# A mixture-of-experts kernel: the last expert's rows given to the tokens by one-hot products, the other rows' loads issued ahead of its work, and the row buffer zeroed in the mixer

## The chip, the cores and the metric

The kernel runs on one core of a Trainium2 chip. The metric is device time in microseconds (us) from launch to end of one execution; three executions of the kernel before gave 2562.1, 2564.21 and 2567.2 us, and the median, 2564.21 us, is the time that a change is held against. All arithmetic is float32, partly as products of split halves.

## What is computed

Two layers act on 512 latent tokens and 256 context tokens of 1024 columns. Each layer has a token mixer (windowed attention, a Fourier mix, a retention with chunks, three gates and an output projection) and then a mixture of 32 experts, of which each token uses two. The last layer drops the context tokens. Cut to the part that the change touches:

```python
def expert_ffn(xb, e, w_g, w_u, w_d):
    return (silu(xb @ w_g[e]) * (xb @ w_u[e])) @ w_d[e]        # 1024 -> 512 -> 1024

def hier_moe(h, ...):
    grp = argmax(h @ w_rg + b_rg)                              # one of 4 groups
    top_v, top_i = top_k(expert_logits_of_group, 2)            # two of its 8 experts
    w = p_grp * softmax(top_v)
    out[token] += w * expert_ffn(h[token], expert)             # for both experts of a token
x = x + g2 * hier_moe(modulate(rmsnorm(x), ...))
return rmsnorm(x, norm_final)                                  # after the second layer
```

## The kernel before, in words

The kernel is written with a tile framework that orders each engine's instructions by a schedule simulated ahead of time; the source gives the order in which the work has priority. Buffers come from pools: `unit` (20 buffers of 8 KB a partition, for weights, token rows and more), `W2` (7 of 2 KB), `raws` (4 of 2 KB), and eight PSUM banks in pools of three (`psm`), two (`pss`), two (`pst`) and one (`pso`). SP issues nearly all loads, in order.

In each layer the mixer comes first. Its projections read weights in pieces of 256 KB through `split_load` (L234). Around L760 attention ends, and the Fourier tables `t2` are loaded (L762 and L763).

Then comes the expert part. The router ranks the experts by their load, so that rank 0 has the most tokens. `SLOTS` (L31) gives each rank a fixed number of blocks of 32 rows; a pair makes one block of 64 rows. Rank 31 has one block of 32 in both layers. `prep` (L1067) builds a one-hot matrix of a rank's tokens, gets token numbers and weights by small products (`slots`, L1025), and gathers the tokens' rows from DRAM on the POOL queue. `wload` (L955) loads an expert's six weight tiles of 1 MB each, four of gate and up and two of down; a load is issued when the fourth load before it has landed.

The loop at L1198 goes over the experts in the order `seq` (L1191 to L1195): first rank 0 (ranks 0 and 1 in the second layer), then some of the smallest, then a small and a large one in turn, so that the last has a middle rank and two slots. For each block it runs `hidden` (L1143: gate and up products, then Silu on ACT and a product on DVE), `turn` of the block before (L1158: transposes and a copy), `take` of the block after (L1131), and `give` of the block before (L1167: the down product, the scaling by the routing weight and by `g2`, and a scatter of the 64 or 32 rows to `y_d` in DRAM, on the POOL queue). Each token has two rows in `y_d`, and both are written exactly once. After the loop the last block is turned and given (L1215), and in the first layer the decay tables of the second layer's retention are made (`decay_logs` and `decay_tables`, L1216 to L1218).

At L1222 stands a loop with a count read from memory, which gives a rank that has more tokens than slots its further blocks. With these inputs it is passed over. Every engine has a part in it.

At L1251 to L1268, for each tile `t` of 128 tokens (six in the first layer, four in the second): SP loads both rows of each token from `y_d` (`yb`, 1 MB), DVE adds them and adds the sum to `x`, ACT squares, DVE and POOL make the reciprocal root (`rstd_x`, L1270), and DVE scales. In the first layer the scaled rows go on to the second layer's `make_h` (L247), whose transposes stand at L259; in the second the result is stored to `out`.

Of the kernel before, what the change touches and what calls it, by code (L numbers as in the profile page):

```python
# [14 lines left out]
AF = mybir.ActivationFunctionType  # L15
# [10 lines left out]
NE = 32  # L26
# [4 lines left out]
SLOTS = ([4, 6, 5, 4, 4, 4] + [3] * 6 + [2] * 16 + [1] * 4, [3] * 2 + [4] * 4 + [3] * 3 + [2] * 8 + [1] * 15)  # L31
# [30 lines left out]
def tile_backbone(ctx: ExitStack, tc: tile.TileContext, a: dict, out: bass.AP, stop=None, dbg=None):  # L62
# [36 lines left out]
    def pst():  # L99
        return ps(pstr, "tr")  # L100
# [296 lines left out]
    def layer(l, xt_l, xt_c):  # L397
# [363 lines left out]
        o_tiles("F")  # L761
        t2 = unit("t2")  # L762
# [404 lines left out]
        def give(aT, sz, wd, di, ws):  # L1167
# [14 lines left out]
            DVE.scalar_tensor_tensor(y, p2[:, 0:n], ws[:, 0:1], g, op0=OP.mult, op1=OP.mult)  # L1182
            s = POOL.indirect_dma_start(out=y_d[l].rearrange("r (a c) -> (r a) c", c=n),  # L1183
# [7 lines left out]
        seq, rest = list(range(NS)), list(range(NS, NE))  # L1191
# [4 lines left out]
        last, xT = None, None  # L1196
        pre += [prep(r) for r in seq[NS:2]]
        for i, r in enumerate(seq):  # L1198
            e = r if r < NS else nc.values_load(oi[0:1, r:r + 1], engines=[ET.SP], min_val=0, max_val=NE - 1)
            w = wload(e) if i else first  # L1200
# [4 lines left out]
            for j, (xg, sz, di, ws) in enumerate(blocks):  # L1205
# [8 lines left out]
                last = (sg, sz, wd, di, ws)  # L1214
        give(turn(*last[:2]), *last[1:])  # L1215
        if full:  # L1216
            decay[1] = decay_logs(1)
            decay[1] = decay[1], decay_tables(*decay[1][0:2])  # L1218
# [31 lines left out]

        xs = {}  # L1251
        yv = y_d[l].rearrange("(k r h) c -> r k (h c)", k=2, h=2)
        for t in TL:
            yb = unit("yb").rearrange("p (k c) -> p k c", k=2)
            SP.dma_start(yb, yv[(t - t0) * 128:(t - t0) * 128 + 128])  # L1255
            x = xt[t]
            DVE.tensor_tensor(yb[:, 0], yb[:, 0], yb[:, 1], op=OP.add)  # L1257
            DVE.tensor_tensor(x, x, yb[:, 0], op=OP.add)
            if full and t >= 2:
                SP.dma_start(x_d[(t - 2) * 128:(t - 1) * 128, :], x)  # L1260
            ss = rstd_x(x, yb[:, 1])
            xs[t] = yb[:, 0]
            if full:
                DVE.tensor_scalar(xs[t], x, ss, None, op0=OP.mult)
            else:
                DVE.scalar_tensor_tensor(xs[t], x, ss, nf, op0=OP.mult, op1=OP.mult)  # L1266
                SP.dma_start(out[(t - 2) * 128:(t - 1) * 128, :], xs[t])
# [196 lines left out]
```

## Time and profile before

| | us |
|---|---|
| median of three executions | 2564.21 |
| lowest, highest | 2562.1, 2567.2 |
| the profiled execution's own time | 2571.19 |
| its span, first to last instruction | 2569.4 |
| TensorE busy (matmul) | 2354.5 (92%) |
| VectorE busy | 1019.1 (40%) |
| ScalarE busy | 576.1 (22%) |
| GpSimd busy | 544.6 (21%) |
| moved by DMA | 595.21 MB, mean 232 GB/s |
| mean granted TensorE clock | 0.956 |

PE is TensorE's matmuls and PEld its weight loads, DVE is VectorE, ACT ScalarE, POOL GpSimd, and SP the engine that issues most transfers; a q behind an engine's name is its queue, where it issues transfers and waits. The shares are means over stages with different limits: in the mixers PE is busy and the DMA engines are mostly idle, in the expert parts both are busy, and at the end of each expert part neither is. A matmul's end is modelled in the profile, so a busy PE may be a waiting one. The span is 1.8 us shorter than the profiled execution's own time, and that time is 7.0 us above the median of the three.

### The profile page before, as it was taken

The page shows a single profiled execution, that of the slowest core. Times are in us where ns is not written, and L with a number is a line of the kernel's source. Part 1 is how long each engine was busy: PE and PEld are TensorE (multiplying, and loading weights), DVE is VectorE, ACT ScalarE, POOL GpSimd, SP SyncE. Part 2 cuts the span into 40 slices and gives each one's busy share as a digit, 9 for nine tenths or more (in the row PEclk, how much of TensorE's full clock was granted, in tenths as well). Part 3 has the DMA queues.
Part 4 walks back from the last instruction along what each step waited for, and adds up shares of the span by engine and source line. Part 5 has one row for each costly group of instructions (what it writes and reads, how often), then busy time and mean ns, then how long its engine had stood idle before and what let it go on. Part 6 is the DMA issues. An engine that isn't in the chain of part 4 may idle for free. (4 is left out here: it accounts for less than half of the span.)

```text
span 2569.4 us, 44175 instructions
## 1 busy us (share of the span) xinstructions
PE 2354.5 (92%) x17341; PEld 1543.7 (60%) x17341; DVE 1019.1 (40%) x3007; ACT 576.1 (22%) x1269; POOL 544.6 (21%) x454
## 2 busy tenths in 40 slices
PE   5999999999999799999999599999999789988774
PEld 3788766888889643434443388768888643343221
DVE  5534555424334732333332745464334622221112
ACT  4222345211222201111110432354233200000000
POOL 0223233001223321111211233241122321121111
PEclk8999999999999799999999799999999799998887
DMA  7433100444333699899999522211335699999996
GB/s 272 166 128 134 64 26 29 164 144 176 107 112 111 238 405 408 348 362 389 416 419 405 199 62 71 69 38 42 98 95 195 240 405 417 412 409 414 409 419 249
DMA packets 130018, 595.21 MB, mean 232 GB/s; under 512 B 20972, under 2 KB 22084, under 8 KB 74256
## 3 DMA queue, kind: packets, MB, share of 16 engines
q1 hardware_dynamic: 115472, 562.70, 57.2%
q0 software_dynamic: 13376, 26.27, 2.7%
q8 instruction: 138, 2.26, 0.4%
q10 hardware_dynamic: 960, 3.39, 0.4%
q14 instruction: 72, 0.59, 0.1%
HBM read 580.53 MB, written 28.25 MB: 237 GB/s over the span
## 5 line engine op out<-in xcount | busy, mean ns | idle before, releaser
L1149 PE MATMUL mm<-w_gu,xT 128*32 128x256 f32 (+1 forms) x3776 | 569.7, 507 | 72.2 <-DMA w_gu<-in_w_gu_dram 69.5
L1149 PEld LDWEIGHTS mm<-w_gu,xT 128*32 128x32 f32 (+1 forms) x3776 | 194.9, 127 | 379.6 <-issue 236.1
L239 DVE TENSOR_TENSOR hl<-raw,hl 128x512 fp32r<-128x512 f32 x248 | 185.9, 751 | 270.9 <-ACT hl L238 270.1
L276 PE MATMUL mm<-hH,hl 128*128 128x512 f32 x720 | 286.2, 399 | 0.2 <-DVE shuf L317 0.2
L277 PE MATMUL mm<-hL,hl 128*128 128x512 f32 x720 | 284.1, 395 | 0.0
L278 PE MATMUL mm<-hH,hl 128*128 128x512 f32 x720 | 281.9, 392 | 1.2 <-DVE hl L239 1.2
L1174 PE MATMUL mm<-w_d,aT 128*32 128x256 f32 (+1 forms) x1888 | 267.8, 488 | 8.8 <-DVE aT L1164 7.7
L1183 POOL DMA_INDIRECT y_d<-y,gd x87 | 87.7, 1008 | 725.9 <-DVE y L1182 540.2
L238 ACT CAST hl<-raw 128x512 fp32r<-128x512 f32 x248 | 153.7, 621 | 384.8 <-PE mm L278 213.8
L1154 ACT ACTIVATE act<-mm 128x256 f32<-128x256 f32 (+1 forms) x87 | 30.1, 346 | 900.6 <-PE mm L1149 857.8
L1174 PEld LDWEIGHTS mm<-w_d,aT 128*32 128x32 f32 (+1 forms) x1888 | 92.8, 124 | 157.2 <-issue 122.2
L1155 DVE TENSOR_TENSOR act<-act,mm 128x256 f32<-128x256 f32 (+1 forms) x87 | 32.2, 370 | 367.0 <-ACT act L1154 364.9
L278 PEld LDWEIGHTS mm<-hH,hl 128*128 128x128 f32 x720 | 135.8, 189 | 30.7 <-DVE hl L239 1.6
L276 PEld LDWEIGHTS mm<-hH,hl 128*128 128x128 f32 x720 | 135.7, 189 | 28.6 <-issue 1.9
L277 PEld LDWEIGHTS mm<-hL,hl 128*128 128x128 f32 x720 | 136.1, 189 | 27.2 <-issue 2.6
L276 PE MATMUL mm<-hcH,hl 128*128 128x256 f32 x440 | 127.2, 289 | 1.4 <-DVE shuf L317 0.7
L1056 POOL DMA_INDIRECT xg<-h_d,gd x87 | 91.3, 1050 | 164.6 <-issue 82.4
L278 PE MATMUL mm<-hcH,hl 128*128 128x256 f32 x440 | 126.0, 286 | 0.0
L277 PE MATMUL mm<-hcL,hl 128*128 128x256 f32 x440 | 126.0, 286 | 0.0
L623 POOL TENSOR_SCALAR sa<-sa,den 128x512 f32<-128x512 f32 (+2 forms) x40 | 71.1, 1779 | 159.7 <-DVE den L621 76.2
L816 POOL TENSOR_TENSOR yl<-yl,sg 128x512 f32<-128x512 f32 x32 | 54.8, 1711 | 196.0 <-DVE sg L815 195.9
L276 PEld LDWEIGHTS mm<-hcH,hl 128*128 128x128 f32 x440 | 84.7, 192 | 10.2 <-issue 2.2
(401 smaller groups left out, 3891.3 us busy)
## 6 DMA issues: line engine op xcount, KB each, us to landing
w_gu<-in_w_gu_dram SPq DMA_DIRECT2D x256, 1024.0 KB
w_d<-in_w_d_dram SPq DMA_DIRECT2D x128, 1024.0 KB
raw<-in_w_in_dram SPq DMA_DIRECT2D x200, 256.0 KB
wada<-in_w_ada_dram SPq DMA_DIRECT2D x48, 1024.0 KB
raw<-in_w_br_dram SPq DMA_DIRECT2D x48, 256.0 KB
yb<-y_d SPq DMA_DIRECT2D x10, 1024.0 KB
raw<-in_w_out_dram SPq DMA_DIRECT2D x32, 256.0 KB
h_d<-hb POOLq DMA_DIRECT2D x10, 512.0 KB
```

What stands on the lines that cost most here:

```text
L238: ACT.copy(hl[:, 0], r)
L239: DVE.tensor_tensor(hl[:, 1], r, hl[:, 0].bitcast(F32), op=OP.subtract)
L276: PE.matmul(o[:, 0:n], wh, h[kc], start=kc == 0, stop=False)
L277: PE.matmul(o[:, 0:n], wh, lo[kc], start=False, stop=False)
L278: PE.matmul(o[:, 0:n], wl, h[kc], start=False, stop=kc == 7)
L623: POOL.tensor_scalar(S[:, 1, 0:W], S[:, 1, 0:W], den[:, 1:2], None, op0=OP.mult)
L816: POOL.tensor_tensor(y, y, sg, op=OP.add)
L1056: POOL.indirect_dma_start(out=xg, out_offset=None, in_=h2_d[l].rearrange("r (a c) -> (r a) c", c=sz * 8), in_offset=bass.IndirectOffsetOnA ...
L1149: PE.matmul(p1[q * sz:q * sz + sz, 0:n], xT[:, k * sz:k * sz + sz], w[:, q * n:q * n + n], start=k == 0, stop=k == 7, skip_group_check=True)
L1155: DVE.tensor_tensor(sv, sv, pv[:, :, 1, :], op=OP.mult)
L1174: PE.matmul(p2[q * sz:q * sz + sz, 0:n], aT[:, j * 128 + q_ * sz:j * 128 + q_ * sz + sz], w[:, q * n:q * n + n], start=k == 0, stop=k == 3 ...
L1183: s = POOL.indirect_dma_start(out=y_d[l].rearrange("r (a c) -> (r a) c", c=n), out_offset=bass.IndirectOffsetOnAxis(ap=di, axis=0), in_=y, ...
```

## The change

The last rank, 31, gets one block of 64 slots in place of 32 and is taken out of the expert loop. Its weights are loaded behind the loop, as the next six loads in line. Its hidden and down products run behind the counted loop, and its 64 scaled rows stay on chip: a one-hot matrix of the rank's slots (`oh4`), transposed (`place`), multiplies them into PSUM, where the second row of each token is added by a product with the identity. DVE adds the token's first row from `yb`, and then the PSUM halves, to `x`. In every second tile of the second layer both rows go through the identity. The loads of `yb` are issued for all tiles ahead of this work. Since rank 31's rows of `y_d` are no longer written, all of `y_d` is set to zero from a zeroed buffer in the mixer, in front of the load of `t2`. The decay logs and tables move into the loop, at its iterations 26 and 28. In the first layer the scaling moves from DVE to ACT and the stores of `x` from SP to POOL.

```diff
-SLOTS = ([4, 6, 5, 4, 4, 4] + [3] * 6 + [2] * 16 + [1] * 4, [3] * 2 + [4] * 4 + [3] * 3 + [2] * 8 + [1] * 15)
+SLOTS = ([4, 6, 5, 4, 4, 4] + [3] * 6 + [2] * 16 + [1] * 3 + [2], [3] * 2 + [4] * 4 + [3] * 3 + [2] * 8 + [1] * 14 + [2])
...
         o_tiles("F")
+        zero = W2("zero")
+        POOL.memset(zero, 0.0)
+        SP.dma_start(y_d[l].rearrange("(k p) c -> p k c", p=128), bmid(zero, y_d[l].shape[0] // 128))
         t2 = unit("t2")
...
-        seq, rest = list(range(NS)), list(range(NS, NE))
+        seq, rest = list(range(NS)), list(range(NS, NE - 1))
...
+        seq.append(NE - 1)
...
-        for i, r in enumerate(seq):
+        for i, r in enumerate(seq[:-1]):
...
+            if full and i == NE - 6:
+                decay[1] = decay_logs(1)
+            if full and i == NE - 4:
+                decay[1] = decay[1], decay_tables(*decay[1][0:2])
+        wl = wload(number(NE - 1))
         give(turn(*last[:2]), *last[1:])
-        if full:
-            decay[1] = decay_logs(1)
-            decay[1] = decay[1], decay_tables(*decay[1][0:2])
...
+        for t in TL:
+            ybs[t] = unit("yb").rearrange("p (k c) -> p k c", k=2)
+            SP.dma_start(ybs[t], yv[(t - t0) * 128:(t - t0) * 128 + 128])
+        place = []
+        for lo in range(0, NP, 4):
...
+            DVE.tensor_tensor(oh.rearrange("p (t q s) -> p t q s", t=n, q=2),
+                              PR[:, t0 + lo:t0 + lo + n, NE - 1].unsqueeze(2).unsqueeze(3).broadcast_to(sh),
+                              iota1.unsqueeze(1).unsqueeze(1).broadcast_to(sh), op=OP.is_equal)
+            for j in range(n):
+                PE.transpose(tp[:, j * 128:j * 128 + 128], oh[:, j * 128:j * 128 + 128], ident)
...
+        (_, sz, _, ws), = pre[0]
+        yl = rows(turn(hidden(xT, sz, wl[:4]), sz), sz, wl[4:], ws)
...
+            pb = [psm(), psm()] if i % 2 == 0 else [pss(), pss()]
+            both_ = not full and i % 2
+            for j in range(2):
+                for k in ((0, 1) if both_ else (1,)):
+                    PE.matmul(pb[j], ident, yb[:, k, j * 512:j * 512 + 512], start=k == 0 or not both_, stop=False,
+                              skip_group_check=True)
+            for q in range(2):
+                qs = slice(q * 64, q * 64 + 64)
+                PE.matmul(pb[q], place[i][qs], yl[qs], start=False, stop=True, skip_group_check=True)
+            if not both_:
+                DVE.tensor_tensor(x, x, yb[:, 0], op=OP.add)
+            for j in range(2):
+                js = slice(j * 512, j * 512 + 512)
+                DVE.tensor_tensor(x[:, js], x[:, js], pb[j], op=OP.add)
             ss = rstd_x(x, yb[:, 1])
             xs[t] = yb[:, 0]
             if full:
-                DVE.tensor_scalar(xs[t], x, ss, None, op0=OP.mult)
+                if t >= 2:
+                    POOL.dma_start(x_d[(t - 2) * 128:(t - 1) * 128, :], x)
+                ACT.activation(xs[t], x, AF.Copy, scale=ss)
```

`rows` is the part of `give` ahead of the scatter, made a function of its own.

## Rows read from the trace of the kernel before

**Rows 1.** The page: granted TensorE clock and DMA share in 40 slices.
```profile
PEclk8999999999999799999999799999999799998887
DMA  7433100444333699899999522211335699999996
```
**Rows 2.** Windows, first layer's end: window, length, engines busy, clock, DMA share, GB/s.
```profile
1405.00:1410.00 5.00, 3.31 (x17) 1.05 (x16) 0.00 (x0) 0.00 (x0) 0.00 (x0) 1.00 1.00 404
1410.00:1412.00 2.00, 1.58 (x10) 0.44 (x8) 0.00 (x0) 0.00 (x0) 0.00 (x0) 1.00 0.78 328
1412.00:1414.00 2.00, 2.00 (x12) 0.62 (x10) 0.42 (x1) 1.02 (x3) 0.00 (x0) 1.00 0.20 78
...
1431.00:1436.00 5.00, 0.00 (x0) 0.00 (x0) 4.37 (x6) 2.15 (x3) 0.03 (x1) 0.50 1.02 409
...
1456.00:1461.00 5.00, 3.14 (x19) 2.63 (x19) 2.60 (x7) 1.75 (x4) 1.80 (x2) 0.84 0.99 347
```
**Rows 3.** Windows, second layer's end, columns as in the group above.
```profile
2526.00:2528.00 2.00, 1.83 (x10) 0.69 (x12) 0.00 (x0) 0.00 (x0) 0.00 (x0) 1.00 0.65 270
2528.00:2530.00 2.00, 2.00 (x12) 0.66 (x10) 0.42 (x1) 0.39 (x1) 0.00 (x0) 1.00 0.16 66
...
2540.00:2545.00 5.00, 0.00 (x0) 0.00 (x0) 0.00 (x0) 0.00 (x0) 0.00 (x0) 0.50 0.61 232
```
**Rows 4.** Waits of SP's queue: line, releaser, us in total, times, longest.
```profile
SPq L763 <- DVE olA L244: 38.8, 1, 38.8
...
SPq L381 <- PE mm L1174: 10.6, 1, 10.6
...
SPq L1222 <- DMA y_d<-y,gd: 8.6, 3, 8.1
```
**Rows 5.** Timeline, second layer's end: start, length, engine, line, operation, idle before.
```profile
2526.17 1.94 PE L1149 MATMUL mm<-w_gu,xT 128*64 128x512 f32 x8 [0.28 <-SPq L1222]
...
2528.57 0.42 DVE L1155 TENSOR_TENSOR act<-act,mm 128x256 f32<-128x256 f32 x1 [11.12 <-ACT act L1154]
...
2531.47 0.44 PE L1162 MATMUL tr<-cp,act 128*128 128x128 f32 x2
...
2532.73 3.65 PE L1174 MATMUL mm<-w_d,aT 128*64 128x512 f32 x16 [0.82 <-DVE aT L1164]
...
2536.43 0.75 DVE L1182 SCALAR_TENSOR_TENSOR y<-mm,wsl,g 128x512 f32<-128x512 f32 x1 [3.76 <-PE mm L1174]
2538.32 0.98 POOL L1183 DMA_INDIRECT y_d<-y,gd  x1 [4.71 <-issue]
2540.71 2.84 SPq L1255 DMA_DIRECT2D yb<-y_d  x4
2546.40 1.23 DVE L1257 TENSOR_TENSOR yb<-yb 128x1024 f32<-128x1024 f32 x1 [9.22 <-DMA yb<-y_d]
2547.66 1.22 DVE L1258 TENSOR_TENSOR xl<-xl,yb 128x1024 f32<-128x1024 f32 x1
...
2562.14 1.28 DVE L1266 SCALAR_TENSOR_TENSOR yb<-xl,ssn,g 128x1024 f32<-128x1024 f32 x1 [0.66 <-POOL ssn L143]
```
**Rows 6.** Timeline, first layer's end: first token tile, first transposes, last tile's scaling.
```profile
1433.29 1.22 DVE L1258 TENSOR_TENSOR xc<-xc,yb 128x1024 f32<-128x1024 f32 x1
...
1438.28 0.69 PE L259 MATMUL tr<-cp,yb 128*128 128x128 f32 x2 [17.08 <-DVE yb L1264]
...
1458.77 0.75 DVE L1264 TENSOR_SCALAR yb<-xl,ssn 128x1024 f32<-128x1024 f32 x1 [0.67 <-POOL ssn L143]
```
**Rows 7.** First layer's loop: a timeline row of a 32-row block, then a window.
```profile
935.79 1.93 PE L1174 MATMUL mm<-w_d,aT 128*32 128x256 f32 x32 [0.17 <-DVE aT L1164]
...
947.00:964.00 17.00, 15.48 (x266) 9.21 (x260) 7.66 (x38) 1.34 (x4) 5.08 (x5) 0.85 1.02 412
```
**Rows 8.** Windows, first layer's mixer, late attention; columns as in the second group.
```profile
400.00:420.00 20.00, 20.00 (x136) 13.23 (x135) 11.24 (x51) 10.71 (x34) 7.45 (x5) 1.00 0.00 1
```
**Rows 9.** Lines: direct stores issued by POOL, busy us, mean ns.
```profile
L870 POOL DMA_DIRECT2D h_d<-hb x10 | 6.2, 617 | 0.9 <-DVE perm L1085 0.6 <-DVE pen L891 0.3
```

More of the change, by code (lines that the diff above doesn't have):

```diff
@@ L1165, in turn, with rows @@
             return aT
-        def give(aT, sz, wd, di, ws):
+        def rows(aT, sz, wd, ws):
             nq, n, ns = 128 // sz, sz * 8, sz // 32
@@ L1182, in give @@
             DVE.scalar_tensor_tensor(y, p2[:, 0:n], ws[:, 0:1], g, op0=OP.mult, op1=OP.mult)
+            return y
+        def give(aT, sz, wd, di, ws):
+            y, n = rows(aT, sz, wd, ws), sz * 8
             s = POOL.indirect_dma_start(out=y_d[l].rearrange("r (a c) -> (r a) c", c=n),
@@ L1196, in layer, with number @@
         last, xT = None, None
+        seq.append(NE - 1)
+        def number(r):
+            return r if r < NS else nc.values_load(oi[0:1, r:r + 1], engines=[ET.SP], min_val=0, max_val=NE - 1)
         pre += [prep(r) for r in seq[NS:2]]
-        for i, r in enumerate(seq):
-            e = r if r < NS else nc.values_load(oi[0:1, r:r + 1], engines=[ET.SP], min_val=0, max_val=NE - 1)
-            w = wload(e) if i else first
+        for i, r in enumerate(seq[:-1]):
+            w = wload(number(r)) if i else first
             wg, wd = w[:4], w[4:]
@@ L1248, in layer @@
             give(turn(hidden(take(gather(gi, 0, 64), 64), 64, wg), 64), 64, wd, di[:, 0:1], ws[:, 0, :])
-        xs = {}
[L1252 to L1260, printed above, removed]
+        yv = y_d[l].rearrange("(k r h) c -> r k (h c)", k=2, h=2)
@@ new lines, in layer @@
+        ybs = {}
+        for t in TL:
[3 more added lines that the diff above has]
+        for lo in range(0, NP, 4):
+            n = min(4, NP - lo)
+            oh, tp = W2("oh4", n * 128), pst()
+            sh = [128, n, 2, 64]
+            DVE.tensor_tensor(oh.rearrange("p (t q s) -> p t q s", t=n, q=2),
[3 more added lines that the diff above has]
+                PE.transpose(tp[:, j * 128:j * 128 + 128], oh[:, j * 128:j * 128 + 128], ident)
+            pl = W2("place", n * 128)
+            ACT.copy(pl, tp[:, 0:n * 128])
+            place += [pl[:, j * 128:j * 128 + 128] for j in range(n)]
@@ new lines, in layer @@
+        (_, sz, _, ws), = pre[0]
+        yl = rows(turn(hidden(xT, sz, wl[:4]), sz), sz, wl[4:], ws)
+        xs = {}
+        for i, t in enumerate(TL):
+            yb, x = ybs[t], xt[t]
+            pb = [psm(), psm()] if i % 2 == 0 else [pss(), pss()]
[12 more added lines that the diff above has]
+                DVE.tensor_tensor(x[:, js], x[:, js], pb[j], op=OP.add)
```

## The prediction

> **What bounds the kernel now.** I read the page's slices first, then windows around the end of each expert part, then the timeline there, then who waited for whom. The slices show two expert parts in which the DMA engines are full, and mixers in which they are nearly idle [rows 1]. At the end of each expert part the fullness stops: in the first layer the DMA share falls from 1.00 to 0.78 and 0.20 as the last weights land, about 1411 to 1414 [rows 2], in the second between 2526 and 2530 [rows 3]. From there a serial chain runs alone. In the second layer [rows 5]: last quarter of the hidden product to 2528.11, down products to 2536.38, scaling to 2537.18, scatter at 2538.32, loads of the token rows issued at 2540.71, first sum at 2546.40, first finished `x` at 2548.88, last scaling ending at 2563.42. The first layer's first `x` is finished at 1434.51, PE gets its first transposes at 1438.28 after 17.08 us of idleness, and the last tile is scaled at 1459.52 [rows 6]. The change works on these two tails, and what it can give lies there.
>
> **What the counted loop does to the plan.** Between the loads of the last weights and the token rows stands the counted loop. SP stood in it up to 8.1 us for a scatter to land [rows 4]; the last quarter of the hidden product is shown as released by SP's part of it at 2526.17 [rows 5], the moment at which the last gate and up tile landed: SP stood in it for that load too. Though passed over, it lets no engine by until what was issued ahead has landed. In the new order the last expert's weights are issued ahead of it and its products stand behind it. So these products no longer run while the weights come in, three quarters of the hidden product fall out of the cover they had, and what is won is that the token rows load while the products run. That is my forecast's centre.
>
> **The second layer's tail, step by step.** The loop lets go when the loads ahead of it on SP have landed: if that is only the gate and up tiles, 2526.2, if all six, up to 2530 [rows 3, 5]. The schedule of the new order is not shown; I take the middle, 2528.7. Leaving it costs 1.1 us, from the scaling's end to the scatter behind it, 2537.18 to 2538.32 [rows 5] (bounds 0.3 and 2). So products start at 2529.8. The whole hidden product is four quarters of 1.94, 7.8 us. PE has then been idle some 12 us, from the previous expert's down product, and the rows show what an idle PE gets: clock 0.50, 1.2 GHz, after 2540 and at 1431 to 1436, and 0.84 once PE works densely at 1456 to 1461 [rows 2, 3]. I add 2 us (bounds 0, and 7.8 if the lower level lasts throughout): 2539.6. From the hidden product's end to the product on DVE 0.9, transposes to down product 1.26, down product to scaled rows 4.45 [rows 5], 6.6 in all: 2546.2. A product of 512 columns, two of them side by side, takes 3.65 / 4 = 0.91 [rows 5]; the one-hot pair is one of these, an identity pair is two, 1.8, which may be done while PE waits for the copies. I take 0.9 for the pair and nothing for the first identity (bounds 0 and 1.8): 2547.1. With a margin of 0.9 for tiles' order, 2548.0. DVE adds two PSUM halves, each like the scaling's 0.75: 2549.5. That is 0.6 us later than the 2548.88 of before. The token rows are not late: 5.7 us from issue to first sum, with products of 16 us to cover it [rows 5]. After the first `x` DVE has 3 × 1.5 of sums left and 4 × 1.43 of scaling and small steps, 10.2, in place of 14.5 (2548.88 to 2563.42), since both sums of `yb` moved ahead of the wait. PE's 2.7 a tile (1.8 + 0.9) is about as long. With the last square and root uncovered I take 11: 2560.5, a gain of 2.9 us.
>
> **The first layer's tail.** Weights 1413 in the middle [rows 2]; plus 1.1, 9.8 and 6.6, and 1.8 and 1.5 for products and sums, gives 1433.8. Rank 31's larger block adds something earlier: the loop's small ranks now include one of 64 rows where four of 32 stood, 1.9 us more of down product (3.65 against 1.93) and nearly four of hidden product [rows 5, 7]. In that place PE was stalling on weights, clock 0.85 with the DMA share at 1.02 [rows 7], so the hidden part is covered, and I charge 1.8 (bounds 0 and 5.5). First `x` 1435.6 against 1434.51. Five more tiles at PE's 2.7 are 13.5, the root and scaling 3.8 (1434.51 to 1438.28), and I add 2 for the transposes and casts of the next layer in between: 1454.9 against 1459.52. Before, DVE carried two sums, the scaling and those casts; now ACT has the scaling. Gain 4.6 us, which PE, busy from there to the next expert part, passes on to the end. For the tables' move I count nothing: DVE and ACT idle in most of the loop, 0.00 to 1.02 of 2 to 5 us [rows 2].
>
> **The zeroes.** 6.3 MB in the first layer and 4.2 in the second, at the some 400 GB/s of full windows [rows 2] 16 and 11 us of all DMA engines. The buffer is the next one of its pool after attention's last rotation, so I expect the write late in attention, where the DMA share is 0.00 and PE full [rows 8]. SP is standing 38.8 us for `t2`'s buffer there [rows 4], so nothing but weight pieces loaded well ahead is queued behind. I charge 0.2 (bounds 0 and 15, the transfer right ahead of `t2`). The load for the decay tables makes SP stand 10.6 us at the end of the loop now [rows 4]; moved into the loop it stands ahead of weight loads, of which four are in flight, about 10 us. I charge 0.3 (bounds 0 and 6).
>
> The stores of `x` go from SP to POOL. POOL's direct stores show 0.617 us each [rows 9], four of them 2.5 us, between roots that leave it idle, so nothing. The Trainium skill, page DMA: Bandwidth & Descriptors, section Issuing engine by pattern, says a simple store belongs to SP and that the hardware path is generally faster. By that rule the sum would be 2.5 us worse, at 2560; no row has the same store on both queues.
>
> **Sum.** 2.9 + 4.6 − 0.2 − 0.3 = 7.0 us. The profiled execution's own time, 2571.19 (span 2569.4 and 1.8 around it), becomes 2564.2. It stands 7.0 above the median of 2564.21, so the same gain gives 2557.2: I predict 2557.
>
> **Rivals.** *The loop doesn't catch the products.* If the schedule puts the last expert's products in front of the loop, they keep their cover: rows scaled about 2536 and, the loads coming behind the weights, the first `x` near 2540, 9 us earlier than before, plus the 4 of shorter sums; about the same in the first layer. Some 2540. Against it: the products need buffers behind those of the loop in the same pools. *All six loads and every margin.* Letting go at 2530 and 1414.5, an identity pair uncovered in each layer, 4 us for the front of the loop: the gain is spent, 2564. *Slower: the clock.* If PE stays at 1.2 GHz through hidden, transposes and down product in both layers, each loses 7.8 − 2 + 4 = 9.8 us more. 19.6 − 7 is 12.6, giving 2577. It decides from about 3.5 us more of delay in each layer, that is, if the lower level holds some 7 us longer than I allow. For it speaks the long 0.50 at 2540 and at 1431; against it, that PE had little or no work there [rows 2, 3].
>
> **How the numbers follow.** The forecast, 2551 to 2562, has 0.57; products ahead of the loop, 0.08; gain spent, 0.22; slower, 0.13. Held from the unknown landing, zeroes and clock together, the range 2548 to 2570 leaves out the first rival and half of the slow one, under 2 in 10. A measurement of this kernel tells about 0.2%, 5.1 us, from no change. Below 2559.1 lie four fifths of the forecast, 0.45, and the first rival, 0.08: 0.53. Above 2569.3 lie the slow rival, 0.13, and a tail of the second, 0.02: 0.15. The rest, 0.32, lies between.
>
> **What would show it.** The last expert's hidden product in one piece of 8 to 11 us behind the counted loop, its first part at clock 0.50, with the DMA engines on token rows at the same time, would bear out the centre; matmuls of it spread over the weight landings would refute it. The distance from the last weight landing to the first `x` should be about 20 us in both layers, and from there to the last scaling 11 us in the second. The zero write should lie in a window where the DMA share was near nothing, and the Fourier products should start no later after attention. Wrong would make it a zero write next to the load of `t2`, PE idle in the mixer, or loads that pause in the loop at iterations 26 to 29.

## The result, and the profile after

The changed kernel took 2584.06 us (2575.44 to 2588.27) where the kernel before took 2563.89 us beside it: ratio 1.0074 [1.0056, 1.0092], a loss of about 19 us by that ratio where a gain of 7 was forecast. Measured again, in four executions beside some of the experiments, it was 12.4 us slower (2577.97 against 2565.61), ratio 1.0058 [1.0039, 1.0077]. The profiled execution spans 2581.7 us, against 2569.4.

The page of the changed kernel, clock and DMA share in 40 slices, answers to [rows 1]:

```profile
PEclk9999998999999799999999999999999799998898
DMA  7434130445333699899999522231335799999995
```

The 7 that the clock had at the first layer's tail (1413 to 1477 us) is gone, PE has work there now. One digit is lower, the 8 at 387 to 452 us, where the kernel before has 9; and the last DMA digit is 5 in place of 6. Where the time went is read from the issue times of SP's weight loads and last stores, which cut the span into stages:

| stage (us) | before | after | difference |
|---|---|---|---|
| start to the first expert weight of the first layer | 836.0 | 840.8 | +4.8 |
| first to last weight issue, first layer | 569.5 | 570.4 | +0.9 |
| from there to the first weight issue of the second layer (tail and mixer) | 568.0 | 569.0 | +1.0 |
| first to last weight issue, second layer | 547.5 | 547.2 | -0.3 |
| from there to the issue of the last store | 42.4 | 48.1 | +5.7 |

The second layer's tail in the timeline of the changed kernel answers to [rows 5]; the last weight is issued at 2527.5 (at 2521.1 before), so 6.4 us are to be taken off when the two are laid side by side:

```profile
2528.77 0.98 POOL L1190 DMA_INDIRECT y_d<-y,gd  x1 [3.85 <-DVEq L1235]
2538.33 2.50 SPq L1268 DMA_DIRECT2D yb<-y_d  x4
2538.68 8.35 PE L1152 MATMUL mm<-w_gu,xT 128*64 128x512 f32 x26 [10.99 <-DMA w_d<-in_w_d_dram]
...
2547.55 1.93 PE L1152 MATMUL mm<-w_gu,xT 128*64 128x512 f32 x6
2549.41 3.70 PE L1291 MATMUL sc<-yb,cp 128*128 128x512 f32 x8
2549.93 0.42 DVE L1158 TENSOR_TENSOR act<-act,mm 128x256 f32<-128x256 f32 x1 [4.72 <-ACT act L1157]
2552.95 0.38 PE L1165 MATMUL tr<-cp,act 128*128 128x128 f32 x2
2557.43 1.98 PE L1291 MATMUL mm<-yb,cp 128*128 128x512 f32 x4
2557.55 0.75 DVE L1185 SCALAR_TENSOR_TENSOR y<-mm,wsl,g 128x512 f32<-128x512 f32 x1 [3.76 <-PE mm L1177]
2559.34 1.13 PE L1295 MATMUL mm<-y,place 64*128 64x512 f32 x4
2560.50 1.29 DVE L1300 TENSOR_TENSOR xl<-xl,mm 128x512 f32<-128x512 f32 x2 [2.20 <-PE mm L1295]
...
2574.24 1.28 DVE L1308 SCALAR_TENSOR_TENSOR yb<-xl,ssn,g 128x1024 f32<-128x1024 f32 x1 [0.67 <-POOL ssn L143]
```

The hidden product stands in one piece behind the counted loop, as forecast, and the token rows load beside it. But the products begin 11.2 us after the last weight issue, PE does 3.70 us of identity products between the hidden product and the transposes (the product on DVE was ready at 2550.35), and the last scaling ends 13.7 us after the first finished `x` (2561.79). These identity products are the four of the second tile, in which both rows go through the identity (`sc`; a product of 512 columns counts as x2 in these rows); the two of the first tile stand at 2557.43.

The first layer's tail, answering to [rows 6] (last weight issue 1411.2, before 1405.5):

```profile
1412.46 0.98 POOL L1190 DMA_INDIRECT y_d<-y,gd  x1 [3.86 <-DVEq L1235]
1423.32 3.39 SPq L1268 DMA_DIRECT2D yb<-y_d  x6
1423.47 7.88 PE L1152 MATMUL mm<-w_gu,xT 128*64 128x512 f32 x26 [12.09 <-issue]
...
1433.73 1.99 PE L1291 MATMUL sc<-yb,cp 128*128 128x512 f32 x4
1435.97 0.37 ACT L1280 COPY place<-tr 128x256 f32<-128x256 f32 x1 [3.41 <-PE tr L1278]
1436.24 0.39 ACT L1157 ACTIVATE act<-mm 128x256 f32<-128x256 f32 x1
1437.88 0.44 PE L1165 MATMUL tr<-cp,act 128*128 128x128 f32 x2 [1.95 <-DVE act L1158]
...
1444.33 1.13 PE L1295 MATMUL mm<-y,place 64*128 64x512 f32 x4
1446.70 0.68 DVE L1300 TENSOR_TENSOR xc<-xc,mm 128x512 f32<-128x512 f32 x1
...
1458.90 0.66 PE L259 MATMUL tr<-cp,yb 128*128 128x128 f32 x4
...
1462.92 1.15 ACT L1306 ACTIVATE yb<-xl,ssn 128x1024 f32<-128x1024 f32 x1 [0.34 <-POOL ssn L143]
```

The windows (window, length, engines busy, clock, DMA share, GB/s) of both tails answer to [rows 2, 3]:

```profile
1418.00:1420.00 2.00, 0.00 (x0) 0.00 (x0) 0.00 (x0) 0.00 (x0) 0.00 (x0) 0.50 0.48 202
1421.00:1422.00 1.00, 0.00 (x0) 0.00 (x0) 0.00 (x0) 0.00 (x0) 0.00 (x0) 0.50 0.06 25
1424.00:1426.00 2.00, 2.00 (x6) 0.48 (x4) 0.18 (x2) 0.00 (x0) 0.00 (x0) 0.50 0.78 217
1428.00:1431.00 3.00, 3.00 (x14) 0.83 (x10) 1.23 (x1) 0.00 (x0) 0.00 (x0) 1.00 1.02 418
...
2534.00:2536.00 2.00, 0.00 (x0) 0.00 (x0) 0.00 (x0) 0.00 (x0) 0.00 (x0) 0.50 0.31 126
2536.00:2537.00 1.00, 0.00 (x0) 0.00 (x0) 0.00 (x0) 0.00 (x0) 0.00 (x0) 0.50 0.06 25
2545.00:2550.00 5.00, 5.00 (x20) 1.66 (x17) 0.28 (x2) 0.97 (x2) 0.00 (x0) 1.00 1.00 406
```

Most of the weights' bytes have passed by about 1420 and 2536. A trickle follows, 25 GB/s, and only then do the engines go on. Two things stand ahead of the loop: the last weights, and the scatter of the expert before the last, which POOL issues right after them (2528.77, 1412.46), so that it travels behind them. The trace marks when each of the 16 parts of a transfer lands. The scatter's last part landed at 1419.66 and 2535.67, 7.2 and 6.9 us after its issue; the DMA view has the first of these, and 6.6 us for the scatter just before it in the second layer:

```profile
y_d<-y,gd POOLq DMA_INDIRECT x2, 7.2
y_d<-y,gd POOLq DMA_INDIRECT x2, 6.6
```

The last weight tile's last part landed at 1422.16 and 2537.85, 11.0 and 10.4 us after its issue and some 2 us after the scatter. The trickle is this tile: from 1420 to 1422.5 and from 2535.5 to 2538 the only queue with packets is `q1`, that of the weights, and none are on `q0`, where a lone scatter of the kernel before (2532.62) has all its 80 packets:

```profile
q1 hardware_dynamic: 13, 0.07, 7.0%
q1 hardware_dynamic: 8, 0.05, 4.7%
```

So it is the last weight tile that lets the loop go, and PE's row at 2538.68 names it as releaser (`w_d<-in_w_d_dram`). In the second layer the engines' waits in the loop have the same order: for the scatter until 2535.70, then for the weight until 2537.86.

Two more windows show the write of the zeroes, and the slice with the 8; the third is that slice in the kernel before:

```profile
362.00:378.00 16.00, 16.00 (x87) 10.66 (x86) 8.85 (x34) 9.34 (x26) 4.63 (x4) 1.00 1.03 370
420.00:440.00 20.00, 19.23 (x84) 11.82 (x82) 8.88 (x40) 8.46 (x27) 7.04 (x4) 0.58 0.00 1
420.00:440.00 20.00, 18.46 (x147) 12.07 (x147) 12.88 (x59) 13.45 (x39) 9.43 (x8) 1.00 0.15 51
```

The write lies at 362 to 378 us beside a full PE, as forecast. At 423 to 440 us the granted clock is 0.50 while PE is busy throughout, where the kernel before had 1.00. That explains some 7 of the 12.3 us between the two profiled executions (up to there the execution of the changed kernel was 2.5 us ahead, behind it 4.8 us late).

### The profile page after: what moved, and what is told of

Read it like the earlier page. It is cut to its first block, busy times and chain, and to the rows that moved or that the text cites. A ratio compares the mean times of both kernels' runs of the same rounds, so it can differ in the third digit from the quotient of the medians.

```text
span 2581.7 us, 44113 instructions
## 1 busy us (share of the span) xinstructions
PE 2402.1 (93%) x17309; PEld 1557.1 (60%) x17309; DVE 1018.9 (39%) x3012; ACT 587.3 (23%) x1280; POOL 533.9 (21%) x458
## 5 line engine op out<-in xcount | busy, mean ns | idle before, releaser
L1152 PE MATMUL mm<-w_gu,xT 128*64 128x512 f32 (+1 forms) x3712 | 574.6, 513 | 91.4 <-DMA w_gu<-in_w_gu_dram 66.3
L1152 PEld LDWEIGHTS mm<-w_gu,xT 128*64 128x64 f32 (+1 forms) x3712 | 196.2, 128 | 400.9 <-issue 257.1
L276 PE MATMUL mm<-hH,hl 128*128 128x512 f32 x720 | 285.3, 397 | 0.2 <-DVE shuf L317 0.2
L276 PEld LDWEIGHTS mm<-hH,hl 128*128 128x128 f32 x720 | 135.4, 188 | 28.4 <-issue 1.9
L277 PEld LDWEIGHTS mm<-hL,hl 128*128 128x128 f32 x720 | 135.5, 188 | 26.8 <-issue 2.6
L276 PE MATMUL mm<-hcH,hl 128*128 128x256 f32 x440 | 126.6, 288 | 1.4 <-DVE shuf L317 0.7
L276 PEld LDWEIGHTS mm<-hcH,hl 128*128 128x128 f32 x440 | 83.8, 190 | 10.0 <-issue 2.2
```

The lines of the kernel that those rows point to most:

```text
L276: PE.matmul(o[:, 0:n], wh, h[kc], start=kc == 0, stop=False)
L277: PE.matmul(o[:, 0:n], wh, lo[kc], start=False, stop=False)
L1152: PE.matmul(p1[q * sz:q * sz + sz, 0:n], xT[:, k * sz:k * sz + sz], w[:, q * n:q * n + n], start=k == 0, stop=k == 7, skip_group_check=True)
```

## The experiments

All ratios are to the kernel before on the same chip. Stage lengths are in us and come from the issue times in each run's profiled execution, as in the table above; "tail 2" is the last row of it, "end 1" the third, "loop 1" the second. The kernel before has 569.5, 568.0 and 42.4 in its profile; five others with the first layer's order as it was (zero_only, decay_only, slots_only, before_identity, only_second) have 566.0 to 567.5 and 563.9 to 570.3, and 41.9 to 42.4 where the second layer is as it was. The means are 567.2, 567.1 and 42.2.

**Parts of the change alone.**

`zero_only`, the kernel before and

```
+        zero = W2("zero")
+        POOL.memset(zero, 0.0)
+        SP.dma_start(y_d[l]..., bmid(zero, ...))
```

> The kernel before, with the zeroing of y alone added in the mixer (here it does nothing for the result). Theory A, the zero write itself takes the time that was lost in the first layer's attention: the granted clock falls to 0.50 for some 17 us at 420 to 440 us as in the changed kernel, and the time is 5 to 9 us above the kernel before. Theory B, that fall has another cause (chance of the execution, or another part of the change): no fall there, and the time is within 3 us of the kernel before, the write lying at 360 to 378 us with nobody waiting.

Ratio 0.9995 [0.9978, 1.0011]; loop 1 566.0, end 1 563.9, tail 2 42.4. Theory B: the zeroes cost nothing.

`decay_only`, the kernel before with the two lines `decay[1] = ...` moved from behind the last `give` to `i == NE - 6` and `i == NE - 4` in the loop.

> The kernel before, with the logs and tables for the second layer's decay moved into the first layer's loop alone. Theory A: the move is a gain, since the counted loop of the first layer let go only when DVE and ACT had come through the tables (1424.6 us); the token rows are then issued some 3 us earlier, less 1 to 2 us of weight loads held behind the load of the table, so 1 to 3 us faster. Theory B: the held loads cost more than the tail gains, 1 to 6 us slower. Theory C, that of the prediction: 0.3 us, nothing to be seen.

Ratio 0.9994 [0.9982, 1.0005]; loop 1 566.9, end 1 568.2. Theory C. The token rows were issued 24.2 us after the last weight, not earlier than the 20.8 of before.

`slots_only`, the kernel before with

```
-... [2] * 16 + [1] * 4, ... [1] * 15)
+... [2] * 16 + [1] * 3 + [2], ... [1] * 14 + [2])
```

> The kernel before with the changed kernel's list of slots alone: rank 31 gets one block of 64 rows instead of one of 32, in both layers. Theory A, PE is what the first layer's loop waits for, so the larger block's 5.7 us of products (7.8 + 3.65 against 3.9 + 1.93) come through: 3 to 6 us slower, from the first to the last weight issue of the first layer's loop. Theory B, that of the prediction: covered but for 1.8 us, under 2 us slower.

Ratio 1.0011 [1.0000, 1.0023]; loop 1 567.1. PE's idle time from the second expert to the last weight issue fell from 20.1 to 14.7 us and took the larger block in: theory B by the stage. The ratio alone, 0 to 6 us, would not tell the theories apart.

`order_only`, the kernel before with

```
-        seq, rest = list(range(NS)), list(range(NS, NE))
+        seq, rest = list(range(NS)), list(range(NS, NE - 1))
...
+        seq.append(NE - 1)
```

> The kernel before with the changed kernel's order of experts alone: rank 31 comes last instead of second in the loop; slots, scatter and sums as before. Theory A, the order is what made the first layer's loop about 4 us longer in the changed kernel (the slots alone added 0.3 and the decay tables nothing): first to last weight issue of the first layer's loop 521 to 524 us against 516 to 521.5, 2 to 5 us slower in all. Theory B, the loop's length has to do with what follows it (the weights of the last expert issued ahead of the counted loop): 518 to 519, and within 2 us of the kernel before.

Loop 1 574.2, but ratio 1.0008 [0.9994, 1.0022], tail 2 41.5. The stretch between the weights of iterations 9 and 10, where the largest blocks meet, is 28.8 us; it is 20.7 to 24.0 in the seven traces with the old order (mean 22.0) and 22.2 to 29.4 in the eleven with the new one (mean 26.7). The ranges overlap, so the order lengthens the loop in most executions, not in each (theory A for the stage); how much of it reaches the end, 2 us less to 6 us more, the interval leaves open.

`only_second`, the changed kernel with the first layer as before, its slots included:

```
+        if not full:
             zero = W2("zero") ...
...
+        if not full:
             seq.append(NE - 1)
...
-        for i, r in enumerate(seq[:-1]):
+        for i, r in enumerate(seq if full else seq[:-1]):
...
+        if not full:
             wl = wload(number(NE - 1))
...
+        if full:   # sums, stores and scaling of the kernel before
```

> The changed kernel with the first layer as in the kernel before (its slots, order, scatter, sums and stores, no zeroes there); the second layer has the change, and the decay tables stay inside the first layer's loop. Theory A, both layers lose: the second layer's tail is 5 to 7 us longer than before and the rest unchanged, so 4 to 8 us above the kernel before, about half of the changed kernel's loss. Theory B, the loss is the first layer's alone: within 3 us of the kernel before.

Tail 2 is 48.0, the changed kernel's, as theory A has it. The ratio, 1.0061 [1.0044, 1.0077], is more than that tail's 5.8 us (0.22%); in its profile 8 us lie before the first expert, in the same fall of the clock at 425 us. Whether its three other executions had that fall is not known.

**The fall of the clock.** `after_again` is the changed kernel unchanged, `decay_back` the changed kernel with

```
-            if full and i == NE - 6: ...
-            if full and i == NE - 4: ...
+        if full:   # behind give(...)
+            decay[1] = decay_logs(1)
+            decay[1] = decay[1], decay_tables(*decay[1][0:2])
```

> The changed kernel itself, on the chip of these runs. Theory A, the fall of the granted clock to 0.50 at 423 us belongs to the execution that was profiled: not here, and what remains above the kernel before is the loop, the two tails and PE's added work, 12 to 18 us. Theory B, it comes with the change: here again, at 418 to 428 us, and 18 to 24 us above the kernel before.

> The changed kernel with the decay logs and tables back behind the last expert's scatter, ahead of the counted loop, as in the kernel before. Theory A, the move inside the first layer's loop pays: without it the loop lets go 2 to 5 us later, less 1 us of weight loads not held, so 1 to 4 us above the changed kernel. Theory B, it is a cost by the held weight loads: 1 to 4 us below it. This run also shows whether the fall of the granted clock to 0.50 at 423 us, which the profiled execution of the changed kernel had, comes with the change (then it is here too, the time 0.5% or more above the kernel before) or with the execution.

Ratios 1.0058 [1.0039, 1.0077] and 1.0062 [1.0039, 1.0084]. Neither has the fall. `before_identity` (below), which is the kernel before up to the first layer's tail, has it. The windows, first of after_again, then of zero_only, then of before_identity:

```profile
420.00:440.00 20.00, 18.45 (x149) 12.62 (x148) 12.50 (x56) 13.47 (x42) 9.31 (x7) 1.00 0.16 52
```

```profile
420.00:440.00 20.00, 18.45 (x149) 12.77 (x148) 12.56 (x56) 13.45 (x40) 9.30 (x7) 1.00 0.16 52
```

```profile
420.00:440.00 20.00, 19.23 (x87) 11.49 (x85) 8.69 (x41) 9.31 (x28) 6.77 (x4) 0.61 0.00 1
```

Of the 18 traces 11 have the zeroes in the first layer, 3 of them with the fall; 7 have none, 2 of them with it. It belongs to the execution: theory A of after_again. The move of the tables shows no effect in the ratios (1.0062 against 1.0058, each known to some 0.2%). In the one profile of decay_back end 1 is 573.5, in that of after_again 569.4, as theory A of decay_back has it; the ratios don't settle it.

**The counted loop.** `products_ahead`, the changed kernel with

```
         wl = wload(number(NE - 1))
+        (_, sz, _, ws), = pre[0]
+        sg = hidden(xT, sz, wl[:4])
         give(turn(*last[:2]), *last[1:])
+        yl = rows(turn(sg, sz), sz, wl[4:], ws)
...
-        (_, sz, _, ws), = pre[0]
-        yl = rows(turn(hidden(xT, sz, wl[:4]), sz), sz, wl[4:], ws)
```

`after_no_loop`, the changed kernel without `with tc.For_i(0, left, 1)` and its body (rows of overflowing experts are left out); `loop_first`, the changed kernel with that loop moved in front of `seq, rest = ...`; `before_loop_first`, the kernel before with the same move.

> The changed kernel, with the last expert's hidden and down products ahead of the counted loop instead of behind it; the token rows stay behind it. Theory A, the loss at the two tails is the cover that the hidden product lost plus the idle PE's clock: hidden product spread over the weight landings again, token rows issued at about the last weight landing plus 8 us, first finished x in the second layer 3 us earlier than in the kernel before, time 10 to 20 us below the changed kernel and below the kernel before. Theory B, the loss is in the new work behind the products (identity and one-hot products, two PSUM sums, order on PE): time within 6 us of the changed kernel.

> The changed kernel without the counted loop for overflowing experts (left out: that loop, which does no iteration with these inputs). Theory A, the loop as a barrier is what spoils the plan: hidden product spread over the weight landings, token rows loaded right behind the last weights while the down product runs, first x of the second layer some 3 us after the last scaled row, 25 to 35 us below the changed kernel, near 2550. Theory B, the tail is bound by its own new work: under 10 us below the changed kernel.

> The changed kernel with the counted loop for overflowing experts moved from the end of each expert part to its start, in front of the first preparation of slots. Theory A, the loop spoils the change only by where it stands: the tails are those of the kernel without the loop (token rows issued 8 us after the last weight's issue, last output store 34 us after it in the second layer), and the start pays 0 to 5 us a layer, so 14 to 24 us below the kernel before. Theory B, the barrier costs the same wherever it stands, 8 to 12 us a layer at the start: within 5 us of the kernel before.

> The kernel before with the same move of the counted loop alone. Theory A: the last scatter still stands in front of the token rows, so the second layer's tail gains only the loop's own 1 us, the first layer's some 3 us (its loop waited for the decay tables), less 0 to 5 us a layer at the start: between 4 us faster and 6 us slower than the kernel before, so that the change is worth 12 to 22 us once the loop is out of its way. Theory B, the loop was the cost of the tail in the kernel before as well: 12 us or more faster, and the change itself worth little.

| kernel | ratio | loop 1 | end 1 | tail 2 |
|---|---|---|---|---|
| products_ahead | 1.0009 [0.9995, 1.0023] | 570.5 | 562.8 | 45.3 |
| after_no_loop | 0.9911 [0.9886, 0.9937] | 568.5 | 555.1 | 34.4 |
| loop_first | 0.9983 [0.9969, 0.9997] | 576.7 | 553.2 | 34.4 |
| before_loop_first | 1.0062 [1.0042, 1.0082] | 574.1 | 567.8 | 41.9 |

Without the loop the changed kernel is 22.5 us faster than the kernel before, which has the loop. Timeline of after_no_loop, second layer (last weight issue 2505.1):

```profile
2505.83 7.09 PE L1152 MATMUL mm<-w_gu,xT 128*64 128x512 f32 x32
2512.93 2.32 SPq L1240 DMA_DIRECT2D yb<-y_d  x4
...
2518.58 1.96 PE L1263 MATMUL mm<-yb,cp 128*128 128x512 f32 x4
2520.46 1.13 PE L1267 MATMUL mm<-y,place 64*128 64x512 f32 x4
2521.62 1.28 DVE L1272 TENSOR_TENSOR xl<-xl,mm 128x512 f32<-128x512 f32 x2 [1.22 <-PE mm L1267]
```

The hidden product lies beside the landings, the token rows are issued 7.8 us after the last weight, and the first `x` is finished 17.8 us after it; 34.3 in the changed kernel, 27.8 before. With the loop at the start of the part the tails keep this (34.4), but the start pays: from the first weight to that of the second expert in the first layer 58.0 in place of 48.0, from the first to that of the third in the second layer 86.3 in place of 72.5. Both theories of loop_first had a part: A for the tails, B for the price of the barrier. before_loop_first is 16 us slower, outside both its theories: its tails are hardly shorter (567.8 and 41.9), so the loop had cost the kernel before little there, and the start pays far more than the 0 to 5 us a layer of theory A. The two kernels with the loop in front differ by 0.79% (1.0062 less 0.9983), some 20 us: that is the change without a barrier in its tail.

In products_ahead the cover is back and the token rows come 16.6 us after the last weight issue (19.6 before), yet its tail 2 is 2.9 us longer than before. Its timeline (last weight issue 2515.2):

```profile
2531.75 3.19 SPq L1271 DMA_DIRECT2D yb<-y_d  x4
2538.16 3.57 PE L1292 MATMUL mm<-yb,cp 128*128 128x512 f32 x4 [3.12 <-DMA yb<-y_d]
2541.66 1.13 PE L1296 MATMUL mm<-y,place 64*128 64x512 f32 x4
2542.82 1.29 DVE L1301 TENSOR_TENSOR xl<-xl,mm 128x512 f32<-128x512 f32 x2 [3.45 <-PE mm L1296]
```

From the token rows' issue to the first `x` 12.4 us pass, 8.2 before: a PE that was idle does the first tile's identity products in 3.57 us (granted clock 0.50 from 2535 to 2540) where 1.96 is the price at full clock. From there to the end it is 16.3, against 14.5. So each theory held for a half: some 12 us below the changed kernel, as A has it, but not below the kernel before.

**The new sums.** `sums_dve` is the changed kernel with

```
-                    PE.matmul(pb[j], ident, yb[:, k, ...], start=k == 0 or not both_, ...)
-            if not both_:
+            DVE.tensor_tensor(yb[:, 0], yb[:, 0], yb[:, 1], op=OP.add)
             DVE.tensor_tensor(x, x, yb[:, 0], op=OP.add)
```

and `before_identity` the kernel before with, for each tile,

```
+            for j in range(2):
+                pb = psm()
+                PE.matmul(pb, ident, yb[:, 1, j * 512:j * 512 + 512], start=True, stop=True)
```

> The changed kernel with the rows of y summed on DVE (two sums a tile, as in the kernel before) and no identity products; the one-hot products stay. Theory A, the identity products cost the tail: in the second layer they stood 2.6 us in front of the transposes of the last expert and made PE's pitch 3 us a half; without them 4 to 8 us less there and 1 to 4 us less in the first layer, 5 to 12 us below the changed kernel. Theory B, DVE takes the place of PE as the bound: within 3 us of the changed kernel.

> The kernel before, with the identity products of the changed kernel added to its sums (two of 512 columns a tile, their results are not used). Theory A, from the first layer's tail to its next expert part PE is the bound, so each product added there is paid though DVE still does the sums: 6 tiles x 2 products of 1.0 us, 6 to 13 us slower, all of it between the last weight issue of the first layer and the first of the second, and the second layer's tail within 2 us. Theory B, that of the prediction's sum: the products lie beside PE's idle time at the tail and cost 0 to 3 us.

sums_dve: ratio 1.0043 [1.0026, 1.0059], tail 2 44.2, 3.9 us shorter than after; end 1 572.2, no shorter. before_identity: ratio 1.0014 [1.0000, 1.0029], end 1 566.4. What PE did in end 1 (idle: no product running; work: busy time less half of what was busy at 0.50, that is, in time at full clock):

| kernel | end 1 | idle | busy at 0.50 | work |
|---|---|---|---|---|
| before | 568.0 | 33.9 | 17.4 | 525.4 |
| before_identity | 566.4 | 24.0 | 12.6 | 536.1 |
| after | 569.0 | 19.0 | 3.4 | 548.3 |
| sums_dve | 572.2 | 26.9 | 23.7 | 533.4 |
| products_ahead | 562.8 | 12.4 | 4.2 | 548.3 |
| after_no_loop | 555.1 | 6.9 | 3.4 | 546.5 |

The change gives PE 22.9 us more to do in this stage. It takes 14.9 us of idleness away and, with less work at 0.50, 7.0 us of slower clock; what is left is the 1.0 us by which the stage is longer. The identity products alone (10.7 in before_identity) lie mostly in idle time and the stage is no longer: theory B there, though the ratio, 0 to 7 us, is wider than that. In the second layer they cost 3.9 us: theory A there. As a whole sums_dve can't be told from the changed kernel (1.0043 against 1.0058 and 1.0062, each known to some 0.2%).

**What beats both.** `split`, the changed kernel with only the hidden product ahead of the loop:

```
         give(turn(*last[:2]), *last[1:])
+        (_, szl, _, wsl), = pre[0]
+        sgl = hidden(xT, szl, wl[:4])
...
+        yl = rows(turn(sgl, szl), szl, wl[4:], wsl)
```

`split_dve1` adds the edit of sums_dve in the second layer, `split_dve` in both.

> The changed kernel with the last expert's hidden product ahead of the counted loop and its transposes and down product behind it. Theory A, the barrier is harmful only where work stands on the wrong side of it: the hidden product is then covered by the weight landings, the loop lets go at the last scatter's landing some 11 us after the last weight's issue, and the down product covers the loads of the token rows; first finished x of the second layer 19 to 22 us after the last weight's issue (27.8 in the kernel before, 34.3 in the changed one), last output store 36 to 39 us after it; with the longer loop of the first layer 6 to 13 us below the kernel before. Theory B, the down product ahead of the barrier is what ties it (the engines arrive late in any order): like the kernel with all products ahead, within 3 us of the kernel before.

> The split kernel (hidden product of the last expert ahead of the counted loop, the rest behind it), with the second layer's rows of y summed on DVE and no identity products there; the first layer keeps them. Theory A, what the second layer's tail still loses is the order on PE: three and a half microseconds of identity products stood between the scaled rows and the first one-hot product; without them the last output store comes 37 to 39.5 us after the last weight's issue (41.3 with split, 42.4 before), 2 to 4 us below split and 4 to 9 us below the kernel before. Theory B, DVE's two sums a tile take PE's place: 41 to 43, no gain over split.

> The same with the sums on DVE in both layers. Theory A, in the first layer PE is the bound from the tail to the next expert part, and leaving out 15 us of identity products pays there: 2 to 8 us below the kernel with DVE sums in the second layer alone. Theory B, in the first layer those products lie in PE's idle time, as they did when added to the kernel before: within 2 us of it, or up to 4 us slower because PE idles longer and falls to a granted clock of 0.50.

split: ratio 0.9988 [0.9977, 0.9998], end 1 561.7, tail 2 41.3; split_dve1: 0.9994 [0.9981, 1.0007], 561.6 and 40.7; split_dve: 1.0008 [0.9998, 1.0018], 564.8 and 38.8. split is the only whole kernel besides loop_first whose interval lies under 1, by 3 us. Its second tail (last weight issue 2525.1):

```profile
2525.18 7.09 PE L1152 MATMUL mm<-w_gu,xT 128*64 128x512 f32 x32
2536.01 2.66 SPq L1270 DMA_DIRECT2D yb<-y_d  x4
2539.05 5.86 PE L1177 MATMUL mm<-w_d,aT 128*64 128x512 f32 x16 [0.52 <-DVE aT L1167]
2544.95 0.75 DVE L1185 SCALAR_TENSOR_TENSOR y<-mm,wsl,g 128x512 f32<-128x512 f32 x1 [2.10 <-PE mm L1177]
2546.65 3.60 PE L1292 MATMUL sc<-yb,cp 128*128 128x512 f32 x8
2550.18 1.13 PE L1296 MATMUL mm<-y,place 64*128 64x512 f32 x4
```

The loop lets go at 10.9 us, the time that theory A gave, but at the landing of the last weight tile (10.4) and not at the scatter's. Then it falls short twice: the down product takes 5.86 us for 3.65, since PE had stood still (granted clock 0.67 from 2535 to 2540 and 0.65 from 2540 to 2545), and 3.60 us of identity products, those of the second tile, precede the first one-hot product. With these gone (split_dve1) the tail is only 0.6 us shorter, nearer to theory B of that run. It is not settled: split_dve has the same source for the second layer and a tail of 38.8, as theory A has it. The order on DVE differs: in split_dve1 a sum of another tile stands between the two halves of the first `x`, which is finished 26.8 us after the last weight issue, against 25.8. split_dve as a whole is some 4 us slower than split_dve1 by the medians, with 3.2 us in end 1: theory B of that run.

## Why the prediction was wrong

**The counted loop: right in kind.** The loads of the last weights stood ahead of it and the products behind; hidden took 10.2 us to its end in the first layer and 10.7 in the second (9.8 forecast), the clock was 0.50 for its first part and 1.00 soon after (2545 to 2550: 1.00). The rival with PE at 1.2 GHz throughout, whose 2577 is nearest to the measured time, is refuted as a mechanism. So is that of products ahead of the loop. From the last weight landing to the first `x` it was 23.9 us in the second layer and 25.2 in the first, for the 20 that I named.

**The release: the first term that was too small.** I let the products begin 8.7 us after the last weight issue (2529.8 less 2521.1) and, in the first layer, 8.6; it was 11.2 and 12.3. The step that failed is the landing: "if that is only the gate and up tiles, 2526.2, if all six, up to 2530 [...] I take the middle, 2528.7" (the middle of the two would be 2528.1). The loop waited for all six, and the last part of the last tile landed 10.4 us after its issue (11.0 in the first layer), where 2528.7 allows 7.6. In the kernel before it had landed 9.95 us after its issue as well, at 2531.04; the bound of 2530 was read from the DMA share, 0.16 in the window up to there [rows 3], in which the last part does not show. The way out of the loop was about right: 0.8 and 1.3 us for 1.1. The scatter of the expert before stands in front of the loop too, which I forgot, but it landed 2.2 and 2.5 us ahead of the last weight and set nothing here. The rival *All six loads and every margin* had this step nearly right: 2530 and 1414.5, where the same axis gives 2531.5 and 1416.5.

**The order on PE: the second.** "I take ... nothing for the first identity (bounds 0 and 1.8)". The row shows 3.70 us ahead of the transposes, and for the second tile, with four products, where I had counted two a tile. From hidden's end to the scaled rows it took 8.9 (second layer) and 9.6 us (first; there the copy of the second one-hot transposes on ACT, 1435.97, also stood in front of the activation) in place of 6.6.

**After the first `x`: the third.** 13.7 us for the 11 I took: PE does the identity and one-hot products of a tile in turn with DVE, through two pairs of PSUM buffers, and they take 1.98 + 1.13 us, or 3.70 + 1.13 where both rows go through the identity, for the 2.7 that I counted. The second layer's tail adds up: 2.5 + 0.9 (hidden) + 2.3 + 0.2 (scaled rows to first `x`) + 2.7 = 8.6, which is the forecast gain of 2.9 turned into a loss of 5.7.

**The first layer: the step that failed was its measure.** The same terms ran over here: the first `x` was finished 36.2 us after the last weight issue (1447.38), where the forecast, 1435.6, has 30.1. From there to the last scaling it took 16.7 us for 19.3. I compared the last scaling, 1454.9 with 1459.52, and let PE "pass on" the difference. The last scaling did come 1.1 us earlier, counted from the last weight issue (52.9 against 54.0). But before, PE had begun the next layer's work between the tiles: its first transposes came 32.8 us after the last weight issue, in the changed kernel 47.7 (1458.90), the eleventh product of L276 59.6 against 61.8. Over the whole stage 22.9 us of added work took the place of 14.9 us of idleness and 7.0 us of slower clock. Forecast -4.6, measured +1.0 (569.0 against 568.0).

**The loop.** I charged 1.8 for the slots and 0.3 for the tables. The loop stage shows neither (567.1 and 566.9 against a mean of 567.2), though the interval of slots_only, 0 to 6 us, leaves 1.8 open. I gave no term to the order of experts, which lengthens the loop at the large blocks: 0.9 us in the pair of profiles, 3.2 against the mean, 7.0 in order_only.

**The zeroes** cost nothing and lie where I put them. The stores of `x` on POOL took 0.53 to 0.63 us, and one root stood 0.8 us behind such a store. On SP's queue the same stores took 0.32 to 0.33 us each to issue in the kernel before, but no two runs differ in this alone. The rule of the Trainium skill, page DMA: Bandwidth & Descriptors, section Issuing engine by pattern, that a simple store belongs to SP, decided nothing here.

**What adds up, and what stays open.** Against the mean of the six traces named above the stages of the changed kernel give 3.2 (loop 1) + 1.9 (end 1) - 0.7 (the second layer's loop, 547.2 against 547.9) + 5.9 (tail 2) = 10.3 us, and the second measurement 12.4. The first gave some 19. The fall of the clock at 423 us, which is no part of the change, adds some 7 us where it comes: the profiled execution of 2583.45 has it, that of after_again at 2577.32 does not. That most of the other executions timed first had it too (four of the six are above 2583) is argued from this, not shown; the mean granted clocks, 0.959 to 0.964 in those four against 0.966 and 0.969 in the other two, would fit it.

## What to carry to other kernels

A loop that is passed over is still a barrier in this kernel, and it lets go when the last load or store in front of it has landed. Here that was the last part of the last weight tile, some two microseconds after nearly all of its bytes. Write down on which side each product, load and scatter stands, and let what has cover stay ahead of it. A round trip through memory replaced by products helps only where the engine that takes them has idle time up to the end of the stage; compare that engine's idle time and added work over the whole stage, not the end of one chain. Where a part is hard to place, leave it out in one run: without the barrier the changed kernel was 22 us faster than the kernel before.

## What the runs showed of the hardware

The granted clock fell to 0.50 for 17 to 21 us at 423 to 425 us in 5 of 18 traces, while PE was busy. In the changed kernel PE had stood still for 0.77 us shortly ahead of it, as it had in the kernel before, which kept 1.00. The five need 840.8 to 843.8 us to the first expert weight, the other thirteen 833.9 to 836.1. Small scatters issued while 1 MB weight loads were in flight needed 6.6 to 7.2 us to land, the last one of the kernel before, alone on the queues, 2.4 (2538.32 to 2540.69). The last 1 MB weight load of a layer needed 9.9 to 11.7 us from issue to its last part in the 18 traces; in the second layer of the changed kernel that part came 1.9 us after the fifteenth of the sixteen (2535.96, 2537.85). The empty loop cost some 10 us in the first layer and 14 in the second when it stood at the start of the expert part, more than at the end of it in the kernel before, which the same move made 16 us slower.
